# Output weights split in place ahead of the key/value tiles, up's product 5 in front, down's pieces one tile later: a hybrid decoder layer on one core

## The chip, the cores and the metric

The kernel runs on one core of a Trainium2 chip. A core has five engines that each follow their own fixed list of instructions: TensorE (PE; its weight loads are shown apart as PEld), VectorE (DVE), ScalarE (ACT), GpSimd (POOL) and SyncE (SP), which here only issues transfers. ACT and POOL issue transfers too; the three queues are shown as SPq, ACTq and POOLq. An engine stops at an instruction whose inputs or whose buffer aren't ready, and all that stands behind it on that engine waits with it.

The metric is the device time of one execution in microseconds, the median of the runs.

## The reference

One layer of a decoder with two mixers side by side, for 1,024 prompt tokens and 8 samples of 8 new tokens (1,088 tokens in all, model width 1,024).

```python
hn = rms_norm(x, norm_mix_gain)
proj = hn @ w_in                    # q_r k_r v_r g_r (512 each), q_s (512), k_s, v_s (128 each)
o_r = rms_norm(retention(q_r, k_r, v_r)) * silu(g_r)          # 8 heads, chunks of 128
o_s = sliding_window_attention(rms_norm(q_s), rms_norm(k_s), v_s, sinks)   # 8 query, 2 key/value heads
h = x + concat(o_r, o_s) @ w_out
y = h + square(relu(rms_norm(h, norm_ffn_gain) @ w_up)) @ w_down           # width 4096
```

It returns y, the retention states and the last keys and values of the window. All is float32.

## The kernel before

**Precision.** PE multiplies in a shorter form of float32 (`F32R`). So each operand is split into a high part, rounded by an ACT cast, and a low part, the rest, by a DVE subtraction (for a few weights by POOL), and each product is three matmuls: high by high, high by low, low by high (`mm3`, lines 175 to 178; line 176 to 178 are the three matmuls). All matmuls go through this helper, so they have these lines whatever the stage; the stage is told by the PSUM tile's name: `psq`, `pst`, `psf` in the projections, `rsr`, `pm` in retention, `pso` in the output projection, `psx`, `psy`, `psz` in up, `psd` in down. Splits are done by `wload` (input weights, lines 80 and 82), `halve` (line 792 the cast, 793 the subtraction), `split_space` and others.

**Stages, in order of time.** (1) Load of x, its split `hnh`/`hnl`, and the attention queries `psq` (until some 52 us). (2) The keys and values of attention in nine tiles of up to 128 tokens: `pst` is a tile's 24 matmuls of 128x256; ACT squares it (`hsq`), DVE sums per head (`hr`, 315, 316), POOL raises to the power −1/2 (136), DVE scales (318), forms `kn` (320) and copies the values (`q2v`, 335); PE transposes `kn` (`ptk`, 325); ACT and DVE then form the high and low keys `kk`, `kl` (331, 332), two of each for each tile and batch of heads. The last tile gives `v8` and `k8`. (3) Retention's projections (`psf`, from 82 us), attention, retention. (4) The output projection `pso` for two halves of the tokens (s = 0, 1), interleaved with the last tiles of retention, from some 370 us. (5) The MLP: up in 16 column tiles (fp = 0 to 15) by a Strassen-like scheme with seven products, whose left sides are sums of weight blocks (formed by POOL, split by ACT and DVE) and whose right sides are sums of blocks of the normalised h (`f`, `op`); then down by the same kind of scheme (from 870 us).

**The output weights.** `wo_pair` loads two of the eight row blocks of `w_out` at a time for one half of the columns, 512 KB, into a slot of the ring "raw", and splits each half block into a slot of the ring "wa". Each block is needed in both halves of the tokens, so the whole of `w_out` is loaded and split twice: 16 loads, 32 casts and 32 subtractions.

**Up's first tile.** Four of the seven left sides are split while the output projection still runs (`ready`). `PROD = (1, 2, 6, 5, 7, 4, 3)` is the order of the splits and, with an exception for fp = 0, of the products.

**Down's pieces.** Four of down's weight blocks are split ahead, during up: for fp = 3 to 10, `split_down` loads half a block (tile `pw`, 128 KB) behind the last store of up's result, casts and subtracts it in place, and stores it to scratch.

**What sets the order.** The code says what is computed; a scheduler with a timeline model of its own then places the instructions on each engine's list. `tc.issue_after(x)` tells it to place an instruction behind x. PE, DVE, ACT, POOL and SP run the lists as they stand. A tile pool hands out its slots in a ring, and a new tile's first writer waits for the last reader of the slot.

## Time and profile before

| | |
|---|---|
| runs | 1186.14 us median of 3 (1183.59 to 1189.11) |
| profiled execution | 1186.29 us, of which the span of the instructions is 1184.4 us |
| granted TensorE clock | 1.00 |
| busy | PE 1168.4 us (99%), DVE 832.2 (70%), ACT 512.0 (43%), POOL 489.6 (41%) |
| transfers | 174.69 MB, mean 147 GB/s |

The page of the profile first gives each engine's busy time; with PE at 99% the rest of the span is a handful of waits. The view of waits gives, for an engine and a line, what it waited for: in total, how many times, the longest. A row of the timeline is start, duration, engine, line, operation, out<-in, shape and count; in brackets stand the idle time before it and what ended that. A row of windows gives each engine's busy time in a stretch, then the granted clock, the share of the 16 DMA engines in use and GB/s. A row of groups has the line, engine, operation, names, shapes and count, then busy us and mean ns of one, then the idle time before them and what ended it. Matmuls overlap: one of 128x272 is shown with 0.29 us, but the next starts 0.12 us later.

### The profile page before, as it was taken

To read this page: it belongs to the slowest core of one execution; us is meant where nothing else is said; L and a number is where in the kernel's file an instruction comes from. 1 tells how busy PE (TensorE), PEld (TensorE's weight loads), DVE (VectorE), ACT (ScalarE), POOL (GpSimd) and SP (SyncE) were. 2 spreads that over 40 slices of the span, in tenths; PEclk is the share of its full clock that TensorE was granted. 3 is DMA by queue.
4 is the path that set the end of the run, shared out by engine and by line. 5 is a ranking of instruction groups with operands and counts; after the bars stand their busy time and mean duration, and the time that the engine had idled before them with its cause. 6 is when DMAs were issued, how large, how long until landed. Compare 5 with 4: busy or idle time off the path is not lost.

```text
span 1184.4 us, 23548 instructions
## 1 busy us (share of the span) xinstructions
PE 1168.4 (99%) x9405; PEld 1123.3 (95%) x9405; DVE 832.2 (70%) x1551; ACT 512.0 (43%) x1060; POOL 489.6 (41%) x393
## 2 busy tenths in 40 slices
PE   8999999999999999999999999999999999999998
PEld 7999988989879899999999999999999999999998
DVE  7556868732258779887757666667688787888676
ACT  8343544553234347644434444444642333333231
POOL 0135334332255542466655656667373142053000
PEclk9999999999999999999999999999999999999999
DMA  6221334333625555343454444434795456442215
GB/s 247 73 62 62 97 105 162 103 118 94 188 72 170 185 180 156 113 156 121 148 176 149 156 162 165 170 123 152 240 381 170 148 165 204 150 159 94 76 59 188
DMA packets 106181, 174.69 MB, mean 147 GB/s; under 512 B 12319, under 2 KB 71647, under 8 KB 105815
## 3 DMA queue, kind: packets, MB, share of 16 engines
q1 hardware_dynamic: 92711, 129.04, 32.6%
q10 hardware_dynamic: 10800, 35.23, 9.0%
q0 software_dynamic: 2560, 8.91, 2.4%
q8 instruction: 74, 1.21, 0.4%
q14 instruction: 36, 0.29, 0.1%
HBM read 117.45 MB, written 55.71 MB: 146 GB/s over the span
## 4 chain that ended last, share of the span: by engine, by line
PE 78%; DVE 6%; DMA 6%; POOL 4%; issue 3%; ACT 2%; SPq 0%; POOLq 0%; DVEq 0%; ACTq 0%
PE psd L177 9%; PE psd L176 9%; PE psd L178 9%; PE psx L176 4%; PE psx L178 4%; PE psx L177 4%; PE pst L176 2%; PE pst L177 2%; PE pst L178 2%; PE psz L176 2%; PE psz L178 2%; PE psz L177 2%; PE psf L176 2%; PE psf L178 2%; PE psf L177 2%
## 5 line engine op out<-in xcount | busy, mean ns | idle before, releaser
L176 PE MATMUL psd<-uh,wd_w 128*128 128x272 f32 x896 | 258.1, 288 | 1.1 <-ACT a L1287 0.8
L177 PE MATMUL psd<-uh,wd_w 128*128 128x272 f32 x896 | 259.2, 289 | 0.0
L178 PE MATMUL psd<-ul,wd_w 128*128 128x272 f32 x896 | 257.7, 288 | 0.0
L176 PEld LDWEIGHTS psd<-uh,wd_w 128*128 128x128 f32 x896 | 169.1, 189 | 1.6 <-ACT a L1287 1.0
L178 PEld LDWEIGHTS psd<-ul,wd_w 128*128 128x128 f32 x896 | 168.6, 188 | 0.0
L177 PEld LDWEIGHTS psd<-uh,wd_w 128*128 128x128 f32 x896 | 168.4, 188 | 0.0
L1290 DVE TENSOR_TENSOR a<-a,psd 128x272 f32<-128x272 f32 x248 | 100.9, 429 | 48.8 <-PE psd L178 48.7
L793 DVE TENSOR_TENSOR wu_w<-wu_s,wu_w 128x512 fp32r<-128x512 f32 x64 | 55.3, 868 | 51.0 <-ACT wu_w L792 50.7
L793 DVE TENSOR_TENSOR ul<-ur,uh 128x1088 fp32r<-128x1088 f32 (+1 forms) x57 | 83.7, 1496 | 6.3 <-ACT uh L792 6.3
L792 ACT CAST wd_w<-wd_s 128x512 fp32r<-128x512 f32 x64 | 37.0, 617 | 116.0 <-PE psd L178 98.4
L176 PE MATMUL psx<-op_0h,wu_w 128*128 128x272 f32 x256 | 74.3, 291 | 1.8 <-ACT m L1142 1.8
L176 PE MATMUL psx<-op_1h,wu_w 128*128 128x272 f32 x256 | 74.3, 290 | 0.5 <-ACT m L1142 0.5
L178 PE MATMUL psx<-op_1l,wu_w 128*128 128x272 f32 x256 | 74.1, 289 | 0.0
L178 PE MATMUL psx<-op_0l,wu_w 128*128 128x272 f32 x256 | 74.1, 289 | 0.0
L177 PE MATMUL psx<-op_1h,wu_w 128*128 128x272 f32 x256 | 73.7, 288 | 0.0
L177 PE MATMUL psx<-op_0h,wu_w 128*128 128x272 f32 x256 | 73.7, 288 | 0.0
L1126 DVE SCALAR_TENSOR_TENSOR m<-m,rsf 128x272 f32<-128x272 f32 x96 | 68.8, 717 | 3.2 <-ACT rsf L915 0.5
L792 ACT CAST uh<-ur 128x1088 fp32r<-128x1088 f32 (+1 forms) x57 | 59.7, 1085 | 15.0 <-PE psd L177 10.1
L366 POOL TENSOR_TENSOR sp<-sp,ssp 128x1024 f32<-128x1024 f32 (+1 forms) x16 | 28.6, 1788 | 88.4 <-DVE ssp L365 60.0
L176 PE MATMUL psf<-hnh,wqk_hi 128*128 128x384 f32 (+1 forms) x192 | 63.5, 331 | 0.2 <-DVE qkst L518 0.2
L178 PE MATMUL psf<-hnl,wqk_hi 128*128 128x384 f32 (+1 forms) x192 | 63.1, 329 | 0.0
L177 PE MATMUL psf<-hnh,wqk_lo 128*128 128x384 f32 (+1 forms) x192 | 62.8, 327 | 0.0
(345 smaller groups left out, 3618.0 us busy)
## 6 DMA issues: line engine op xcount, KB each, us to landing
ur<-u_d SPq DMA_DIRECT2D x53, 544.0 KB, 5.0
u_d<-r4t SPq DMA_DIRECT2D x32, 544.0 KB, 4.1
wu_r<-in_w_up ACTq DMA_DIRECT2D x32, 512.0 KB, 4.4
wd_r<-in_w_down ACTq DMA_DIRECT2D x30, 512.0 KB, 6.4
u_d<-r3t SPq DMA_DIRECT2D x32, 408.0 KB, 3.0
y<-in_xY POOLq DMA_DIRECT2D x16, 272.0 KB, 3.3
y_d<-y POOLq DMA_DIRECT2D x16, 272.0 KB, 3.4
yt<-y_d SPq DMA_DIRECT2D x16, 272.0 KB, 3.0
```

Source lines behind the costliest of these rows:

```text
L176: nc.tensor.matmul(ps, lh, rh, start=first, stop=False, skip_group_check=more)
L177: nc.tensor.matmul(ps, ll, rh, start=False, stop=False, skip_group_check=more)
L178: return nc.tensor.matmul(ps, lh, rl, start=False, stop=last, skip_group_check=more)
L366: nc.gpsimd.tensor_tensor(s, s, ss.unsqueeze(2).broadcast_to([P, 4, n]), ALU.mult)
L792: nc.scalar.copy(hi, src)
L793: lo_eng.tensor_tensor(lo, src, hi.bitcast(F32), ALU.subtract)
L1126: nc.vector.scalar_tensor_tensor(t_, src, 0.0, rsf[:, s, h, :], ALU.max, ALU.mult)
L1290: added[i] = nc.vector.tensor_tensor(to, to, ps, ALU.add).ins
```

## The change

Three edits.

**1. The output weights.** Each of the eight row blocks is loaded once (512 KB, `load_out`, issued by SP behind the input weight loads) in the stage of the key/value tiles. It is split there (`split_out`): ACT casts the two halves into a free tile, DVE subtracts in place, so that the loaded tile becomes the low part; POOL issues the stores of both to the scratch tensor `wo_d`. The blocks take three slots in turn (rings "s", "pt", "mh", which attention uses later). Blocks 0 to 2 are loaded and split ahead of the tiles; 3, 4, 5, 6 and 7 behind tiles 2, 3, 4, 7 and 8, their casts placed behind that tile's square and their subtractions behind its `kn`. `wq1`'s weights are loaded ahead of the tiles now. In the output projection `wo_pair` loads the split halves, 512 KB for each half block (32 loads instead of 16), into seven slots (four of the ring "wa", three of "raw") and splits nothing.

**2. Up's first tile.** The splits are made in the order 1, 2, 5, 6, 7, 4, 3, and the products in the order (1, 0), (1, 1), (2, 0), (5, 0), (5, 1), (6, 0), (2, 1), (6, 1), where the first number is the product and the second the half of the tokens. The norm of the second half goes behind (6, 0).

**3. Down's pieces.** `split_down` is now a generator: a piece is loaded in one tile of up and cast, subtracted and stored in the next, the cast placed behind the last square of the tile.

```diff
+    def load_out(m):
+        wo_t[m] = sp.tile([P, 4, 256], F32R, tag="s", name=f"wo_raw{m}", bufs=3).rearrange("p k n -> p (k n)")
+        with tc.issue_after(raw_loads[-1].ins):
+            nc.sync.dma_start(wo_t[m].bitcast(F32), a["w_out"][m])
+    def split_out(m, act, dve):
+        lo = wo_t[m]
...
+        for i in range(2):
+            l_ = lo[:, i * 512 : i * 512 + 512]
+            with tc.issue_after(act) if act else ExitStack():
+                nc.scalar.copy(his[i], l_.bitcast(F32))
+            with tc.issue_after(dve) if dve else ExitStack():
+                nc.vector.tensor_tensor(l_, l_.bitcast(F32), his[i].bitcast(F32), ALU.subtract)
+        if m % 3 < 2:
+            nc.gpsimd.dma_start(wo_d[m][:, 0, :], hi.rearrange("p k n -> p (k n)").bitcast(F32))
+        else:
+            for i in range(2):
+                nc.gpsimd.dma_start(wo_d[m][:, 0, i * 512 : i * 512 + 512], his[i].bitcast(F32))
+        nc.gpsimd.dma_start(wo_d[m][:, 1, :], lo.bitcast(F32))
-    w = wload(a["w_in"][2], 8, "wkv", "v")
+    w, w_q1 = (wload(a["w_in"][i], 8, n, "v") for i, n in ((2, "wkv"), (1, "wq1")))
+    for m in range(3):
+        load_out(m)
+    for m in range(3):
+        split_out(m, None, None)
+    for m in range(3, 6):
+        load_out(m)
     for t in range(9):
...
+        m = {2: 3, 3: 4, 4: 5, 7: 6, 8: 7}.get(t)
+        if m:
+            split_out(m, act, dve)
+        if m in (4, 5):
+            load_out(m + 2)
...
     def wo_pair(s, m, half):
-        raw = mw.tile([P, 1024], F32, tag="raw", name=f"wo{half}{s}_{m}_raw", bufs=3)
         c0 = 512 * (half == "a")
-        nc.sync.dma_start(
-            raw.rearrange("p (m n) -> p m n", m=2), a["w_out"][m : m + 2, :, c0 : c0 + 512].rearrange("m p n -> p m n")
-        )
         for i in range(2):
-            yield wsplit(raw[:, i * 512 : i * 512 + 512], "wa", f"wo{half}{s}_{m + i}", nc.vector)
+            tag, bufs = ("raw", 3) if len(w_loads) % 7 > 3 else ("wa", 4)
+            w = mw.tile([P, 2, 512], F32R, tag=tag, name=f"wo{half}{s}_{m + i}", bufs=bufs)
+            w_loads.append(nc.sync.dma_start(w.bitcast(F32), wo_d[m + i][:, :, c0 : c0 + 512]))
+            yield w
...
-                PROD, None, "wu0", nc.vector, tags=("wa", "wa", "wa", "wa", "wb", "wb", "wb"), raws=r0,
+                (1, 2, 5, 6, 7, 4, 3), None, "wu0", nc.vector, tags=("wa", "wa", "wa", "wa", "wb", "wb", "wb"), raws=r0,
...
-            order = [(1, 0), (1, 1), (2, 0), (6, 0), (5, 0)] + [(i, 1) for i in (2, 6, 5)] + order[8:]
+            order = [(1, 0), (1, 1), (2, 0), (5, 0), (5, 1), (6, 0), (2, 1), (6, 1)] + order[8:]
...
-        nc.scalar.copy(w[:, 0, :], w[:, 1, :].bitcast(F32))
+        yield
+        with tc.issue_after(last_sq[0]):
+            nc.scalar.copy(w[:, 0, :], w[:, 1, :].bitcast(F32))
...
+    pieces = chain(*(split_down(f, c) for f in range(2, 6) for c in (0, 256)))
     for fp in range(16):
         up(fp)
-        if 2 < fp < 11:
-            split_down(2 + (fp - 3) // 2, 256 * ((fp - 3) % 2))
+        for _ in range((fp > 2) + (fp > 3)):
+            next(pieces, None)
```

The lines of the changed kernel lie further down: `halve` is at 833 and 834, `split_out` at 327 and 329 with its stores at 331, 334 and 335, the keys at 367 and 368, `kn` at 356, `q2v` at 371, down's cast at 1254.

How the rows move on the engines' lists, at three places. The first is DVE at the end of retention. In the order before, the split of the output weights (`woa`, `wor`) stands ahead of the reduce of a tile's output norm (`orrr`):

```order
L718 TENSOR_TENSOR rptr_4162<-rsr_4155,intra 128x512
L793 TENSOR_TENSOR woa_0_4239<-woa_0_raw,woa_0_4239 128x512
L793 TENSOR_TENSOR wor_0_4244<-wor_0_raw,wor_0_4244 128x512
L754 SCALAR_TENSOR_TENSOR state_3397<-state_3396,decs,pur_4074 64x64 x8
L793 TENSOR_TENSOR woa_1_4342<-woa_0_raw,woa_1_4342 128x512
L793 TENSOR_TENSOR wor_1_4345<-wor_0_raw,wor_1_4345 128x512
L718 TENSOR_TENSOR rptr_4276<-rsr_4269,intra 128x512
L617 TENSOR_REDUCE orrr_4094<-osqr_4092 128x8
```

In the order of the change, at the same place:

```order
L759 TENSOR_TENSOR rptr_4237<-rsr_4230,intra 128x512
L818 TENSOR_TENSOR gt_3979<-pm,gt_3979 128x512
L752 TENSOR_TENSOR qkb<-qt_4335,qkb 64x4x128
L647 TENSOR_TENSOR kdr_4133<-pkr_4128,decs 128x512
L752 TENSOR_TENSOR qkb<-qt_4335,qkb 64x4x128
L759 TENSOR_TENSOR rptr_4246<-rsr_4239,intra 128x512
L658 TENSOR_REDUCE orrr_4178<-osqr_4176 128x8
```

The four splits are gone from between the retention rows.

The second place is DVE in the key/value tiles, around the values of the fifth tile (`pst_810` before). Before:

```order
L315 TENSOR_REDUCE hr_837<-hsq_835 128x2
L316 TENSOR_SCALAR hr_837<-hr_837 128x2
L332 SCALAR_TENSOR_TENSOR kk_570<-ptk_754,c_qkg_111,kk_570 64x128 x2
L318 TENSOR_SCALAR hr_837<-hr_837,rst_180 128x2
L320 TENSOR_TENSOR kn_842<-pst_810,hr_837 128x128
L335 TENSOR_SCALAR q2v_278<-pst_810,rst_180 128x128
L332 SCALAR_TENSOR_TENSOR kl_571<-ptk_754,c_qkg_111,kk_570 64x128
```

Of the change, where the tile is `pst_879` and `wo_raw4` and `wo_raw5` are the fifth and the sixth block of output weights:

```order
L329 TENSOR_TENSOR wo_raw4_679<-wo_raw4_679,wo_hi4_870 128x512 x2
L368 SCALAR_TENSOR_TENSOR kl_579<-ptk_717,c_qkg_111,kk_578 64x128
L351 TENSOR_REDUCE hr_906<-hsq_904 128x2
L368 SCALAR_TENSOR_TENSOR kl_579<-ptk_762,c_qkg_111,kk_578 64x128
L352 TENSOR_SCALAR hr_906<-hr_906 128x2
L351 TENSOR_REDUCE hr_962<-hsq_960 128x2
L352 TENSOR_SCALAR hr_962<-hr_962 128x2
L368 SCALAR_TENSOR_TENSOR kk_578<-ptk_807,c_qkg_111,kk_578 64x128
L354 TENSOR_SCALAR hr_906<-hr_906,rst_188 128x2
L368 SCALAR_TENSOR_TENSOR kk_578<-ptk_859,c_qkg_111,kk_578 64x128
L356 TENSOR_TENSOR kn_911<-pst_879,hr_906 128x128
L371 TENSOR_SCALAR q2v_286<-pst_879,rst_188 128x128
```

Two subtractions stand ahead of the tile's chain, the keys of two tiles are interleaved, and the next two subtractions (block 5) follow this `q2v` directly.

The third place is ACT in up, around the first of down's pieces (`pw2_0`). Before:

```order
L1142 COPY m64_1_7061<-psx1_6951 128x272
L792 CAST wu5_w5_7329<-wu5_s5_7294 128x512
L792 CAST wu5_w3_7432<-wu5_s3_7430 128x512
L1211 CAST pw2_0_6945<-pw2_0_6945 128x256
L1142 COPY m74_0_7107<-psx0_6950 128x272
L1142 COPY m74_1_7124<-psx1_6951 128x272
```

Of the change:

```order
L833 CAST wu5_w4_7412<-wu5_r2_7245 128x512
L1182 COPY m15_0_7262<-psx0_7233 128x272
L1167 ACTIVATE r3t4_1_6974<-v4_1_7177 128x272
L1254 CAST pw2_0_6965<-pw2_0_6965 128x256
L848 DMA wu7_r1_7775<-in_w_up 128x1024
L1167 ACTIVATE r124_0_7199<-m64_0_7064 128x272
```

The cast stood ahead of the copies of product 7 of tile 4; it stands behind that tile's last square now, with a load of up's weights behind it.

More of the change, by code (lines that the diff above doesn't have):

```diff
@@ L64, in cload @@
         return t_
+    raw_loads = []
     def wload(src, kk, name, lo_eng="p", parts=2, after=()):
@@ L73, in wload @@
             for q in range(0, 1024, n):
-                nc.sync.dma_start(raw[:, q : q + n], src[:, h * 1024 + q : h * 1024 + q + n])
+                raw_loads.append(nc.sync.dma_start(raw[:, q : q + n], src[:, h * 1024 + q : h * 1024 + q + n]))
                 if after:
@@ L130, in hymba_layer @@
     ms_lo_d = scratch.tile([P, 4, T], F32, name="ms_lo_d")
+    wo_d = [scratch.tile([P, 2, 1024], F32, name=f"wo_d{m}") for m in range(8)]
     y_d = scratch.tile([P, 4, 4, 2, Q], F32, name="y_d")
@@ L304, in hymba_layer @@
     spread(rst, rsb)
-    w = wload(a["w_in"][2], 8, "wkv", "v")
+    wo_t = {}
+    def load_out(m):
[5 more added lines that the diff above has]
+        if m % 3 < 2:
+            hi = sp.tile([P, 2, 512], F32R, tag="pt", name=f"wo_hi{m}")
+            his = [hi[:, i, :] for i in range(2)]
+        else:
+            his = [sp.tile([P, 512], F32R, tag="mh", name=f"wo_hi{m}_{i}") for i in range(2)]
+        for i in range(2):
[4 more added lines that the diff above has]
+                nc.vector.tensor_tensor(l_, l_.bitcast(F32), his[i].bitcast(F32), ALU.subtract)
+        if m % 3 < 2:
+            nc.gpsimd.dma_start(wo_d[m][:, 0, :], hi.rearrange("p k n -> p (k n)").bitcast(F32))
+        else:
+            for i in range(2):
[8 more added lines that the diff above has]
+        load_out(m)
     for t in range(9):
@@ L312, in hymba_layer @@
         sq = sp.tile([P, 128], F32, tag="hsq", name="hsq")
-        nc.scalar.activation(sq, ps[:, :128], AF.Square, scale=rt)
+        act = nc.scalar.activation(sq, ps[:, :128], AF.Square, scale=rt).ins
         r = sp.tile([P, 2], F32, tag="hr", name="hr")
@@ L319, in hymba_layer @@
         kn = sp.tile([P, 128], F32, tag="kn", name="kn")
-        nc.vector.tensor_tensor(
+        dve = nc.vector.tensor_tensor(
             kn.rearrange("p (h d) -> p h d", h=2), ps[:, :128].rearrange("p (h d) -> p h d", h=2),
             r.unsqueeze(2).broadcast_to([P, 2, 64]), ALU.mult,
-        )
+        ).ins
         pt = psB.tile([P, 512], F32, tag="t2", name="ptk")[:, :128]
@@ L947, in hymba_layer @@
         mix[0, "r" + x] = slot(6 + i, F32R, "mixr" + x)[:, : 8 * Q].rearrange("p (k h n) -> p k h n", k=4, h=2)
-    held, mxr, mxrx = {}, None, ExitStack()
+    held, mxr, mxrx, w_loads = {}, None, ExitStack(), []
     for t in range(5):
@@ L1100, in hymba_layer @@
     um = ux.enter_context(pool("u", side="right"))
-    last_sub, last_store = {}, [None]
+    last_sub, last_store, last_sq = {}, [None], [None]
     def up(fp):
@@ L1147, in up @@
                     act(*wait.pop())
-            if fp == 0 and (i, s) == (5, 0):
+            if fp == 0 and (i, s) == (6, 0):
                 norm(1)
-            if fp == 0 and (i, s) == (5, 1):
+            if fp == 0 and (i, s) == (6, 1):
                 norm_spread(1, mm)
@@ L1158, in up @@
                 squared = act(tq("v", s), bk, s, 0, ra[s][:, B21, :])
+                last_sq[0] = squared.ins
                 nc.sync.dma_start(u_d[fp // 2][:, fp % 2, s, :3, :], ra[s])
```

4 lines of the change are left out of this document (2 added, 2 removed).

## The prediction

> **What bounds the kernel now.** First the page's busy times, then the waits of TensorE (PE), because they say how much there is to win at all.
>
> ```profile
> PE 1168.4 (99%) x9405; PEld 1123.3 (95%) x9405; DVE 832.2 (70%) x1551; ACT 512.0 (43%) x1060; POOL 489.6 (41%) x393
> ...
> PE psx L176 <- ACT m L1142: 2.3, 3, 1.0
> ...
> PE rsr L176 <- ACT qkb L710: 1.2, 1, 1.2
> ...
> PE psz L177 <- DVE wu_w L793: 1.1, 1, 1.1
> ...
> PE pm L772 <- DVE mtr L620: 0.5, 1, 0.5
> ```
>
> PE is busy 1168.4 of 1184.4 us, and the change leaves its matmuls as they are (8,113 PE rows, one fewer). So it can win only waits, and 16 us is all the idle time that there is. Any time it costs has to appear as a new wait of PE. Of the waits listed (us in total, times, longest), the change touches four: L1142, L710, L793 in up, and L620. The others stand in the load phase and in the query projection.
>
> **What it removes.** Three edits, three places.
>
> (1) Down's weight pieces. The two long waits on L1142 have one cause:
>
> ```profile
> 600.62 0.29 PE L178 MATMUL psx<-op_0l,wu_w 128*128 128x272 f32 x1
> ...
> 601.16 0.40 ACT L1211 CAST pw<-pw 128x256 fp32r<-128x256 f32 x1 [4.14 <-DMA pw<-in_w_down]
> 601.47 0.67 ACT L1142 COPY m<-psx 128x272 f32<-128x272 f32 x2
> ...
> 601.91 0.39 PE L176 MATMUL psx<-op_0h,wu_w 128*128 128x272 f32 x1 [1.00 <-ACT m L1142]
> ...
> 665.84 0.40 ACT L1211 CAST pw<-pw 128x256 fp32r<-128x256 f32 x1 [3.98 <-DMA pw<-in_w_down]
> ...
> 666.58 0.39 PE L176 MATMUL psx<-op_0h,wu_w 128*128 128x272 f32 x1 [0.84 <-ACT m L1142]
> ```
>
> ScalarE (ACT) stands 4 us on a load, with the copy that frees PE's bank behind the cast; in the order of before the cast is directly ahead of it. In the change's order the cast stands behind the tile's last square, two products further on (of 24 matmuls, 3 us each). The load takes 2.4 to 7.1 us (view of the tile pw, whose first load is issued at 594.1):
>
> ```profile
> L1210 SPq DMA_DIRECT2D pw<-in_w_down x8: 358/383/383, 594.1 to 745.1; - x8
> ...
> DMA to landing us min/median/max: 2.4/3.8/7.1
> ```
>
> so it has landed, by 601.2 at the latest, when the cast comes at some 606. Removed: 1.00 + 0.84 = 1.8 us of waits. Each wait costs some 0.15 more, because a start after a wait comes late: from 600.62 to 601.91 are 1.29 us where two matmuls of 128x272 otherwise start 0.125 apart (160 in 20 us, window row below), so 1.16 are lost for 1.00 shown. Together 2.1. The third L1142 wait lies at 533, before any piece, and stays.
>
> (2) Up's first tile. PE's fourth group of products waits for a split on VectorE (DVE):
>
> ```profile
> 499.85 0.29 PE L176 MATMUL psz<-op_0h,wu_w 128*128 128x272 f32 x1
> ...
> 500.48 0.68 DVE L793 TENSOR_TENSOR wu_w<-wu_s,wu_w 128x512 fp32r<-128x512 f32 x1
> ...
> 501.21 0.39 PE L177 MATMUL psz<-op_0h,wu_w 128*128 128x272 f32 x1 [1.07 <-DVE wu_w L793]
> ```
>
> That split was the fourth, behind two rounds of out-projection operands. Now product 5 is split third and product 6, split fourth, is read only three groups of twelve matmuls after it (4.5 us). Removed: 1.07 shown, 1.24 by starts (501.21 − 499.85 − 0.12).
>
> (3) The output weights. Today their halves are split beside the retention tail, DVE being nearly full there:
>
> ```profile
> 370.00:390.00 20.00, 19.46 (x213) 18.35 (x213) 18.14 (x32) 9.03 (x16) 10.52 (x7) 1.00 0.57 189
> ...
> 480.00:500.00 20.00, 20.00 (x160) 19.92 (x159) 16.11 (x37) 12.16 (x27) 10.74 (x9) 1.00 0.34 111
> ...
> 375.09 1.78 DVE L793 TENSOR_TENSOR wor<-wor_raw,wor 128x512 fp32r<-128x512 f32 x1
> ...
> 380.67 0.68 DVE L617 TENSOR_REDUCE orrr<-osqr 128x8 f32<-128x512 f32 x1
> ...
> 382.45 2.17 POOL L619 TENSOR_TENSOR orrr<-orrr,mhalf 128x8 f32<-128x8 f32 x1 [3.56 <-DVE orrr L618]
> ...
> 385.40 0.33 PE L772 MATMUL pm<-c_ident,mtr 128*128 128x128 f32 x1 [0.54 <-DVE mtr L620]
> ```
>
> (Columns: PE, PEld, DVE, ACT, POOL busy, granted clock, DMA share, GB/s.) Four of these splits stand ahead of the reduce at 380.67 whose result PE wants at 385.4; without them (one is the row at 375.09; at 0.68, what such a split takes in the row at 500.48, and 1.78 they are 2.7 to 7.1 us of DVE) it comes early enough. The wait at 401.46 follows from the same delay: its load of queries stands on SyncE's queue (SP) behind a load that waits for the previous tile's gate. So 0.54 and 1.17 go, 0.7 and 1.3 by starts.
>
> ```profile
> 400.15 1.26 ACT L710 CAST qkb<-qt 64x512 fp32r<-64x512 f32 x2 [3.00 <-DMA qt<-qr_d]
> 401.46 0.39 PE L176 MATMUL rsr<-qkb 128*128 128x256 f32 x1 [1.17 <-ACT qkb L710]
> ...
> 390.17 0.63 SPq L816 DMA_DIRECT2D mixal<-ms_lo_d  x1
> 390.90 0.57 SPq L547 DMA_DIRECT2D qt<-qr_d  x1
> ```
>
> This query load took 9.2 us from issue (390.90) to the cast (400.15), behind two over four times its size (the second is the row at 390.17); moved some 3 us forward it should land by 397 to 398, when PE still has work. Sum of the gains: 2.1 + 1.24 + 0.7 + 1.3 = **5.4 us**; bounds 3.4 (retention's two stay) and 6.0 (the third L1142 wait, 2.3 − 1.84 = 0.46 and its restart, goes too).
>
> **What it adds.** In the out-projection, 8.4 MB more reading (32 loads of 512 KB for 16) in some 100 us, +84 GB/s:
>
> ```profile
> GB/s 247 73 62 62 97 105 162 103 118 94 188 72 170 185 180 156 113 156 121 148 176 149 156 162 165 170 123 152 240 381 170 148 165 204 150 159 94 76 59 188
> ```
>
> The slices there (29.6 us each, the 14th to the 17th: 185, 180, 156, 113) have room below the 381 of the 30th, and seven slots of 32 are some 20 us of PE's work in hand. Taken as nothing; at worst one load comes as late as the queries' did, 1.3 us.
>
> In the front, 16 casts and 16 subtracts of 128x512, 8 loads and 19 stores. The first three blocks (6 casts, 6 subtracts, 6 x 0.68 = 4.1 us) fall where ACT and DVE stand idle:
>
> ```profile
> 40.64 0.62 DVE L275 TENSOR_SCALAR qs<-psq,qg 128x384 f32<-128x384 f32 x1 [4.74 <-ACT sqq L272]
> 40.12 1.15 ACT L272 ACTIVATE sqq<-psq 128x384 f32<-128x384 f32 x3 [8.49 <-PE psq L178]
> ```
>
> These cost nothing. The other five blocks stand among the key/value tiles, and this is the term that decides. There one tile's product may start only when DVE has drained the product three tiles before (q2v), so I follow DVE from the fourth tile's q2v to the last key (k8), by the order of the change and by the groups of before in 60 to 86 us:
>
> ```profile
> L332 DVE SCALAR_TENSOR_TENSOR kl<-ptk,c_qkg,kk 64x128 fp32r<-64x128 f32 x13 | 4.6, 356 | 2.3 <-ACT kk L331 1.7
> L332 DVE SCALAR_TENSOR_TENSOR kk<-ptk,c_qkg,kk 64x128 fp32r<-64x128 f32 x12 | 4.1, 344 | 1.2 <-issue 0.4 <-ACT kk L331 0.4
> L320 DVE TENSOR_TENSOR kn<-pst,hr 128x128 f32<-128x128 f32 x6 | 1.7, 288 | 0.3
> L315 DVE TENSOR_REDUCE hr<-hsq 128x2 f32<-128x128 f32 x6 | 1.7, 286 | 1.9 <-ACT hsq L313 1.8
> L335 DVE TENSOR_SCALAR q2v<-pst,rst 128x128 f32<-128x128 f32 x5 | 1.7, 342 | 0.0
> L318 DVE TENSOR_SCALAR hr<-hr,rst 128x2 f32<-128x2 f32 x6 | 1.4, 228 | 1.7 <-POOL hr L136 1.6
> L316 DVE TENSOR_SCALAR hr<-hr 128x2 f32<-128x2 f32 x6 | 1.2, 197 | 0.2
> ...
> 60.00:68.00 8.00, 8.00 (x69) 8.00 (x68) 5.51 (x21) 3.53 (x11) 2.09 (x3) 1.00 0.00 0
> ...
> 76.00:84.00 8.00, 8.00 (x52) 7.95 (x51) 5.02 (x16) 3.73 (x11) 4.66 (x3) 1.00 0.43 138
> ```
>
> 14 kl, 12 kk, 5 tiles of reduce, two scalings and kn (0.286 + 0.197 + 0.228 + 0.288 = 1.0 each), 4 q2v, and v and k at 0.35: 5.0 + 4.1 + 5.0 + 1.4 + 0.7 = 16.2 us, and the eight subtracts in between at 0.68 make 21.6. PE's work over the same stretch: three tiles of kv (72 matmuls at 8.00 / 69 = 0.116), two query groups and one key group (72 wider ones at 8.00 / 52 = 0.154), seven transposes at 0.12: 8.4 + 11.1 + 0.8 = 20.3. So the work alone is 1.3 us longer than PE's, where before it was 4.1 shorter. On top come the waits of DVE in this stage, on ACT and GpSimd (POOL), 5.5 us before by the releasers named in these rows (1.7 + 0.4 + 1.8 + 1.6). Bounds: below, the splits fill those waits and DVE enters with a lead, 0; above, all waits remain, 1.3 + 5.5, some 7. I take 4, the middle: half of a fill is what a fixed order with five short chains gives. If one pair took the 1.78 us of the row at 375.09, 2.2 more. The Trainium skill (SBUF — State Buffer, "SBUF: two separate sides") says why some are long: a VectorE operation with two SBUF inputs and a GpSimd operation that reads SBUF exclude each other for a whole instruction. The row at 375.09 agrees; by that rule the subtracts of the last two blocks, beside GpSimd's splits of the key weights, would cost up to 1 us more each.
>
> POOL now issues the stores, nine of them ahead of a tile's reciprocal root (0.70 us). A store of half the size costs its queue 0.74:
>
> ```profile
> L842 POOL DMA_DIRECT2D y_d<-y x16 | 11.8, 736 | 20.3 <-DVE y L840 20.3
> L136 POOL TENSOR_TENSOR hr<-hr,mhalf 128x2 f32<-128x2 f32 x9 | 6.3, 698 | 15.8 <-DVE hr L316 14.1 <-DVE q2v L335 1.7
> ```
>
> At 0.74 nine take 6.7 us of a queue that idles 15.8 before the roots, and they stand in the 4 already. SP's loads of blocks 3 to 7 wait for slots, that is for stores; behind them stand the row scales and a key weight, needed 20 us later.
>
> Sum: 1186.3 (the profiled execution, 0.15 above the median of the three) − 5.4 + 4 = 1184.9, against the median **1184.8 us**, −0.1%.
>
> **Rivals.**
>
> *The front is hidden.* If the eight subtracts fill only DVE's gaps, cost 0 to 1: 1186.2 − 5.4 + 0.5 = 1181.3. For it: DVE is busy only 5.51 and 5.02 of 8 us in the two windows above, so 5.4 us of subtracts find 2.5 to 3 us idle in every 8. Against it: the order puts pairs of subtracts directly ahead of kl and q2v. Chance 0.27.
>
> *Stores block the roots.* If a store of 512 KB holds POOL's queue in proportion to its bytes (0.74 x 512 / 272 = 1.39) or longer, the four that stand in a row ahead of the fifth tile's root cost 2.6 us more and the other five 3.3: 1186.2 − 5.4 + 4 + 5.9 = 1190.7; at three times 0.74 (2.2) the extra is 13 and the time 1198. It decides, against the gains, from about 0.9 us of issue. For it: nothing of this size was stored by POOL before. Against it: on SP's queue a transfer of four times the bytes takes 0.63 where the queries' takes 0.57 (rows at 390). Chance 0.13, at 1192. The Trainium skill (SBUF — State Buffer, the same section) calls it a trap: while VectorE runs in a fast two-port mode, GpSimd can't write its descriptors, and a store of 620 ns takes 3,100. Whether the subtracts (512 elements in 680 ns) are of that kind no run here shows.
>
> *Retention's waits stay*, because the queries' load, still beside the two large ones and now a doubled weight stream, lands as late: 1186.2 − 3.4 + 4 = 1186.8. Chance 0.10.
>
> **How the numbers follow.** Forecast 0.50 (its own range 1182.5 to 1188, from a front of 2 to 7). About 0.5%, 5.9 us, is what a measurement can tell from no change; faster than 1180.2 is then the better half of the hidden front and a little more, 0.18; slower than 1192.1 about 0.10; same 0.72. The range leaves out the far ends of the two outer rivals: 1179.5 to 1191.
>
> **What would show it.** ACT waits nowhere on pw, and no L1142 wait near 600 and 665; no psz wait in up's first tile; none on the mtr or the query cast at 385 and 401; new PE waits between 60 and 92 on q2v, kl, v and k, together near 4 us; POOL's stores near 0.74. PE busy must stay at 1168. Wrong would be a front without waits, stores well above 1 us, or a weight load in the out-projection that PE waits for.

## The result: slower by 1.1%, and the profile after

| | before | change |
|---|---|---|
| median of 6 runs each, on the same chip | 1187.32 us (1183.59 to 1189.11) | 1199.59 us (1197.95 to 1202.1) |
| ratio, with its 95% interval | | 1.011 (1.01 to 1.012) |
| profiled execution, and its span | 1186.29, 1184.4 us | 1202.1, 1200.3 us |
| transfers | 174.69 MB | 195.67 MB |

The change costs 12.3 us where 1.5 us of gain were forecast. Its profiled execution is the slowest of its six; a stretch near 500 us, below, makes most of that difference. One run of e5_only3, below, took 1892 us at a granted clock of 0.56, and the median and the ratio given for it are those of its other ten.

First the busy times and the waits of PE in the profile after (the columns are those of the first fence of the prediction):

```profile
PE 1173.4 (98%) x9405; PEld 1128.3 (94%) x9405; DVE 828.6 (69%) x1535; ACT 505.5 (42%) x1046; POOL 503.6 (42%) x411
...
PE ptk L361 <- DVE kl L368: 6.1, 1, 6.1
PE psr L159 <- DVE acc L897: 4.2, 1, 4.2
PE rsr L181 <- DVE qkb L752: 1.7, 1, 1.7
PE pst L179 <- DVE q2v L371: 1.2, 1, 1.2
...
PE ppp L412 <- DVE ptp L454: 1.2, 1, 1.2
...
PE rsr L179 <- ACT qkb L751: 1.0, 1, 1.0
PE scp L441 <- DVE sp L443: 0.9, 2, 0.7
PE pso L179 <- DVE y L880: 0.8, 1, 0.8
PE psf L179 <- DVE v L376: 0.7, 1, 0.7
...
PE psq L179 <- DVE q2v L371: 0.4, 1, 0.4
```

Three of the four waits that the change was to remove are gone from the list: `psx` on ACT's copies (2.3 us before), `psz` on its split (1.1) and `pm` on `mtr` (0.5). (The third wait on `psx`, near 534, which the prediction let stay, is gone here too; in e1 and e5, below, it stays.) The ten lines shown above make 18.2 us in their place. Those on `q2v` and `v`, 2.3 us together, are the waits that the prediction had named for the key/value tiles. Two single waits are 10.3 us. The one on `kl` stands where the prediction had expected some, but this length was in no term of its sum; the one on `acc` was in no term at all.

To see where the time went, I set PE's matmuls of both profiled executions side by side, row by row, and took the difference of their starts:

| stage | lag of the change, us | grows by |
|---|---|---|
| end of the load phase | −0.7 | |
| after the key/value tiles | 10.2 | 10.9 |
| after attention | 12.9 | 2.7 |
| after retention and output projection | 14.6 | 1.7 |
| after up's first tile | 18.9 | 4.3 |
| after down's pieces | 15.8 | −3.1 |
| end | 15.95 | 0.15 |

The −3.1 are three steps: −0.65 at 534, and −1.26 and −1.11 at 600 and 665 where ACT no longer stands on a piece. The 1.7 of retention and output projection is no more than executions differ by: from the first matmul of retention's values to the last of the output projection before takes 209.3 us (285.9 to 495.2), and e5 and e7, which change nothing there, take 211.4 and 211.9.

### The profile page after: what moved, and what is told of

Read it like the earlier page. It is cut to its first block, busy times and chain, and to the rows that moved or that the text cites. A ratio compares the mean times of both kernels' runs of the same rounds, so it can differ in the third digit from the quotient of the medians.

```text
span 1200.3 us, 23623 instructions
## 1 busy us (share of the span) xinstructions
PE 1173.4 (98%) x9405; PEld 1128.3 (94%) x9405; DVE 828.6 (69%) x1535; ACT 505.5 (42%) x1046; POOL 503.6 (42%) x411
## 2 busy tenths in 40 slices
DMA packets 114021, 195.67 MB, mean 163 GB/s; under 512 B 12991, under 2 KB 72319, under 8 KB 113655
## 4 chain that ended last, share of the span: by engine, by line
PE 78%; DVE 4%; DMA 3%; ACT 1%; issue 1%; POOL 0%; ACTq 0%; DVEq 0%; POOLq 0%; SPq 0%
PE psd L180 9%; PE psd L179 9%; PE psd L181 9%; PE psx L180 5%; PE psx L179 5%; PE psx L181 5%; PE psz L180 3%; PE psz L179 3%; PE psz L181 3%; PE pso L179 2%; PE pso L180 2%; PE pso L181 2%; PE pst L179 1%; PE pst L181 1%; PE pst L180 1%; PE psy L179 1%
## 5 line engine op out<-in xcount | busy, mean ns | idle before, releaser
L834 DVE TENSOR_TENSOR wu_w<-wu_s,wu_w 128x512 fp32r<-128x512 f32 x64 | 59.6, 933 | 50.7 <-ACT wu_w L833 50.0
```

What stands on the lines that cost most here:

```text
L834: lo_eng.tensor_tensor(lo, src, hi.bitcast(F32), ALU.subtract)
```

## The key/value tiles: a load behind a store behind a store

These rows of the timeline of the change show what PE waits for when it stands from 75 to 81 us:

```profile
58.22 0.60 POOL L335 DMA_DIRECT2D wo_d<-wo_raw  x1 [2.67 <-DVE kk L368]
...
66.55 0.34 SPq L174 DMA_DIRECT2D rsb<-r_d  x1
68.25 7.47 SPq L315 DMA_DIRECT2D wo_raw<-in_w_out  x2
...
78.97 1.14 ACT L327 CAST wo_hi<-wo_raw 128x512 fp32r<-128x512 f32 x2 [6.17 <-DMA wo_raw<-in_w_out]
80.13 0.36 ACT L367 ACTIVATE kk<-ptk,c_qkg 64x128 fp32r<-64x128 f32 x1
...
80.53 0.35 DVE L368 SCALAR_TENSOR_TENSOR kl<-ptk,c_qkg,kk 64x128 fp32r<-64x128 f32 x1 [7.08 <-ACT kk L367]
...
74.63 0.27 PE L361 MATMUL ptk<-c_ident,kn 128*128 128x128 f32 x1
81.03 0.45 PE L361 MATMUL ptk<-c_ident,kn 128*128 128x128 f32 x1 [6.13 <-DVE kl L368]
```

Read it from the end. PE's transpose waits for a low key on DVE, which waits for the high key on ACT (80.13). That one stands on ACT's list behind the casts of block 6 of the output weights, and these wait 6.17 us for the block's load. SP issues this load at 68.25, because the block takes the slot of block 3, and the store of block 3's low half, issued by POOL at 58.22, lands only at 68.2. So the store takes 10 us and the load behind it 10.6. The load runs beside the stores that were held up with that one: the core moves 396 GB/s from 72 to 76 us, as the windows below show.

Why does a store of 512 KB take 10 us? The view of transfers, cut to short stretches, shows that the transfer engines move almost nothing then:

```profile
DMA packets 918, 0.00 MB, mean 4 GB/s; under 512 B 918, under 2 KB 918, under 8 KB 918
...
DMA packets 7, 0.03 MB, mean 7 GB/s; under 512 B 0, under 2 KB 0, under 8 KB 7
...
q0 software_dynamic: 7, 0.03, 47.0%
...
wo_d<-wo_hi POOLq DMA_DIRECT2D x1, 512.0 KB, 10.5
```

The first row is 56 to 57 us, the others are 60 to 64 (the third: a queue's packets, MB, and the time that they took as a share of the 16 engines; the last: a store issued there, its size, and its us from issue to landing). The 918 packets are the row scales: 1,088 single words of 4 bytes that SP stores to scratch from 54.92 on (`r_d`, lines 172 and 173 of the change), as the kernel before does. In the kernel before nothing else is issued until they have landed, 12 us later, so that the trace of before shows them as a slow but harmless store. The change issues five stores in these 12 us, and the loads that need what the words or the stores leave come after them.

The standstill costs a second time. From the windows of PE in the change (us, PE busy with its matmuls, granted clock, share of the DMA engines, GB/s):

```profile
72.00:76.00 4.00, 2.90 (x25) 1.00 1.03 396
76.00:80.00 4.00, 0.00 (x0) 0.78 0.60 229
80.00:84.00 4.00, 2.57 (x8) 0.50 0.39 149
84.00:88.00 4.00, 4.00 (x22) 0.87 0.46 140
```

After 6 us without a matmul PE comes back at a granted clock of 0.50 and runs at half rate for some 4 us (until about 85, by the 0.87 of the last row), which loses some 1.6 us more: ten matmuls of 128x384 start 0.32 us apart there, where they start 0.17 apart afterwards. The Trainium skill ("TensorE: Matmul & The Clock Gate", "What's actually happening") says that the array's clock falls to half after an idle window of some 3.4 us, and that a busy window of the same length brings it back; the rows agree. The wait of 4.2 us near 520 does the same (granted clock 0.74 and 0.83 in the two stretches of 4 us from 520 on); no shorter one does in this execution.

## The experiments

Each run is compared with the median of before in its own batch (1186.1, 1186.69 or 1186.79 us for the experiments, 1187.32 for the change). Since these medians differ by 1.2 us, differences between batches below 1 us mean nothing.

| run | what | us (runs) | against before | ratio, 95% |
|---|---|---|---|---|
| the change | all three edits | 1199.59 (6) | +12.3 | 1.011, 1.01 to 1.012 |
| e2_front_only | loads and splits of the output weights as before, on top of the new front | 1199.37 (4) | +13.3 | 1.0105, 1.0085 to 1.0124 |
| e3_ring4 | the change, four slots for seven | 1196.84 (4) | +10.7 | 1.008, 1.0058 to 1.0102 |
| e4_rd_rows | the change, row scales stored as rows | 1192.93 (6) | +6.8 | 1.0053, 1.0037 to 1.007 |
| e8_nosub | e4 without ten subtractions (it leaves out forming five blocks' low parts) | 1193.35 (1) | +6.7 | |
| e9_mended | change with rows, four slots, up's first tile as before | 1188.35 (10) | +1.6 | 1.0012, 1.0002 to 1.0021 |
| e1_only23 | edits 2 and 3 alone | 1185.4 (10) | −0.7 | 0.9989, 0.9978 to 1.0 |
| e5_only3 | edit 3 alone | 1184.95 (10) | −1.7 | 0.9985, 0.9974 to 0.9996 |
| e7_wq1 | before, `wq1` loaded ahead | 1187.94 (1) | +1.3 | |
| e6_probe, e10_probe_load | before, with transfers behind the single words | 1188.61, 1185.21 (1 each) | +1.9, −1.6 | |
| r1_again | the change once more | 1199.09 (1) | +12.3 | |

### The edits taken apart: e1_only23, e2_front_only, e3_ring4

e1 has edits 2 and 3 on the kernel before, without the output weights. e2 is the change with its output projection put back:

```diff
+        raw = mw.tile([P, 1024], F32, tag="raw", name=f"wo{half}{s}_{m}_raw", bufs=3)
...
-            tag, bufs = ("raw", 3) if len(w_loads) % 7 > 3 else ("wa", 4)
-            w = mw.tile([P, 2, 512], F32R, tag=tag, name=f"wo{half}{s}_{m + i}", bufs=bufs)
-            w_loads.append(nc.sync.dma_start(w.bitcast(F32), wo_d[m + i][:, :, c0 : c0 + 512]))
-            yield w
+            yield wsplit(raw[:, i * 512 : i * 512 + 512], "wa", f"wo{half}{s}_{m + i}", nc.vector)
```

e3 is the change with `tag, bufs = "wa", 4` for all loads.

> The second and third edits alone (up's first tile and down's pieces), the output weights as before. The forecast's terms say 2.1 us for the pieces and 1.24 for product 5, so 3.3 us faster than before: the waits on the copy near 600 and 665 and the one on the split near 500 are gone, nothing else moves. The rival, that these waits only move to another place of up, gives 0 to 1 us. If the gain is 3 or more, all that the change loses (12 us, or 15 with this gain) comes from the output weights.

> The change, but the output projection loads and splits its weights as before; the splits and stores in front stay, and nothing reads what they store. It parts the loss of the first edit into the front and the later stages. By the two traces the front (52 to 100 us) loses some 10 to 11 us, retention some 2 and the start of up 4. Theory: this kernel keeps the front's loss and drops the other two, so it is about 6 us faster than the change and about 6 slower than before. Rival: the late losses follow from the front (other order on the engines) and not from the doubled loads and the slots; then it is as slow as the change.

> The change with four slots for the split output weights instead of seven; the three slots of the ring raw are left to up's first weight loads, as before. Theory on the wait of 4.2 us of TensorE on the sum of squares near 517 us: up's raw loads came at 491.9 and 494.9 us instead of 471 and 479, because their slots held output weights until TensorE had used them, so GpSimd's sum of weight blocks came at 500 instead of 488 and the residual loads behind it on GpSimd's queue with it. Then this kernel has no such wait and is 4 us faster than the change. Second effect: six loads of 512 KB instead of seven or more stand ahead of the key and query loads of retention, so the waits near 400 us (3 us) get shorter. Rival: the residual loads are late because the doubled stream slows every load; then the wait near 517 stays, and four slots make new waits for weights in the output projection, 2 us or more.

e1 settles that the whole loss comes with edit 1: without it the kernel is level with before. (Edit 1 alone was not run.) It gained less than the 3.3 us that the prediction's terms had promised. The pieces' two waits are gone, and so is the 1.24 us wait in up's first tile. But in the same tile two new ones stand, 1.07 us (`psr` on `acc`, the norm of the second half) and 0.72 us (`psx` on a copy of ACT): edit 2 moved the wait instead of removing it. On e2 I was wrong by 6 us: with the loads and splits of before the kernel is no faster than the change. Its profile has the same 5.4 us wait on `kl` at 74 us and the same growth in attention, and the wait for the query cast is 2.0 us. So the output projection's new loads don't make the loss. e3 gave 1.6 to 2.8 us where 4 were expected; its profile lacks the long wait on `acc` (0.37 us are left of it), which is taken up again below.

### The row scales: e4_rd_rows

PE transposes the scales first, and they go out as nine rows, eight of 512 bytes and one of 256, instead of 1,088 words:

```diff
-        nc.sync.dma_start(r_d[0:1024].rearrange("(t p) -> p t", p=128), rst[:, :8])
-        nc.sync.dma_start(r_d[1024:1088].rearrange("(p t) -> p t", t=1), rst[64:128, 8:9])
+        ps = psB.tile([P, 512], F32, tag="t2", name="psrow")[:9, :128]
+        nc.tensor.transpose(ps, rst[:, :9], ident)
+        rows = nt.tile([P, 512], F32, tag="ntmp", name="rstrow")[:9, :128]
+        nc.vector.tensor_copy(rows, ps)
+        nc.sync.dma_start(r_d[0:1024].rearrange("(t p) -> t p", p=128), rows[:8, :])
+        nc.sync.dma_start(r_d[1024:1088].unsqueeze(0), rows[8:9, 64:128])
```

> The change with one other thing: the row scales are transposed on TensorE and stored as nine rows of 512 bytes instead of 1,088 single words of 4 bytes. In the change's trace five stores of output weights issued from 58.2 to 64.4 us land only at 68 to 75, and the memory is all but idle from 57 to 66 (7 GB/s in 60 to 64); before them the store of single words was issued at 54.9. Before, that store takes 12.3 us from issue to landing. Theory: single words hold up the writes behind them for some 10 us; block 6's load waits for a slot, that is for such a store, and lands at 78.9, where ScalarE's cast of it stands ahead of the keys of the tiles. Then the stores here land within 6 us, ScalarE doesn't wait 6 us for block 6, TensorE's wait of 6.1 us near 75 and the half clock behind it are gone: 8 to 10 us faster than the change. Rival one: GpSimd's own queue is slow to give out its stores; then they land as late as now, and the time stays. Rival two: the memory is full there; the same.

The change's excess fell from 12.3 to 6.8 us, and in the two profiles the lag at the end of the key/value tiles from 10.2 to 3.6. That is less than the 8 to 10 expected: I had counted the front's whole lag. (e4's load phase ends 0.9 us ahead of before's, so its tiles still cost 4.5.) The timeline of SP in this run:

```profile
57.73 0.35 SPq L176 DMA_DIRECT2D r_d<-rstrow  x1
58.14 0.22 SPq L177 DMA_DIRECT2D r_d<-rstrow  x1
59.32 0.35 SPq L178 DMA_DIRECT2D rsb<-r_d  x1
65.07 6.99 SPq L319 DMA_DIRECT2D wo_raw<-in_w_out  x2
```

The load at line 178 reads what the two rows above it store, so they have landed 1.6 us after the first was issued; as words they took 12 us (before) and 11 (the change: 55.4 to 66.55). The store of block 3 now lands in 5.4 us, block 6's load is issued at 65.07 instead of 68.25 and has landed at 71.8 instead of 78.9. ACT's cast stands as before behind a tile's square and ahead of a key, and waits 0.28 us instead of 6.17; first its row, then two of PE's windows of this run:

```profile
71.91 1.14 ACT L331 CAST wo_hi<-wo_raw 128x512 fp32r<-128x512 f32 x2 [0.28 <-DMA wo_raw<-in_w_out]
...
76.00:80.00 4.00, 4.00 (x25) 1.00 0.38 125
80.00:84.00 4.00, 3.56 (x25) 1.00 0.65 201
```

The two windows in which PE stood or ran at half rate have 4.00 and 3.56 us of matmuls now, at the full clock. So the late transfer and its half clock cost 5.5 us by the medians and 6.6 by the profiles. The other way out, to keep the words and cast block 6 behind the keys, was not tried.

### Is it the words? e6_probe and e10_probe_load

On the kernel before, which has nothing behind the words, three transfers of 512 KB were put behind them, a store and a load on POOL's queue and a store on SP's:

```diff
...
+        if t == 2:
+            for v in (pa, pb, pc):
+                nc.gpsimd.tensor_tensor(v[:, 0:2], r, r, ALU.add)
+            nc.gpsimd.dma_start(pb, a["w_out"][1])
+            nc.gpsimd.dma_start(probe_d[0], pa)
+            nc.sync.dma_start(probe_d[1], pc)
```

and in e10 the load `pb` alone.

> The kernel before with three probes right behind the store of the 1,088 single words (issued at 55): a store of 512 KB on GpSimd's queue, a store of 512 KB on SyncE's queue, and a load of 512 KB on GpSimd's queue. What they move is used nowhere. Theory (single words hold up the writes to memory behind them, whatever queue these come from): both stores land only when the words have, 66 to 70 us, some 10 us after their issue, and the load, which only reads memory, lands within 4 us. Rival one, GpSimd's queue is slow: its store and its load are late, SyncE's store isn't. Rival two, all transfers wait: the load is late too. Rival three, GpSimd's stores were late in the change because of the amount stored: all three land within 6 us here.

> The kernel before with one probe behind the store of the 1,088 single words: a load of 512 KB on GpSimd's queue, alone. In the run with three probes the load landed as late as the two stores (71 us, 13 us after its issue), but it stood behind GpSimd's own store. Theory: single words hold up only the writes to memory; alone, the load lands in 3 to 5 us, as such loads do elsewhere. Rival: they hold up reads as well; then it lands at 68 or later, 10 us or more after its issue.

The last row of each view of a tile gives the time from issue to landing, shortest, median, longest. In e6 the tile `probea` (a load at the kernel's start, then the store on POOL's queue), `probec` (the same, with the store on SP's) and `probeb` (the load):

```profile
DMA to landing us min/median/max: 5.9/9.2/12.5
...
DMA to landing us min/median/max: 7.2/9.2/11.2
...
DMA to landing us min/median/max: 13.1/13.1/13.1
```

and the load alone, in e10:

```profile
L321 POOL DMA_DIRECT2D probeb<-in_w_out x1: 734/734/734, 55.7 to 55.7; - x1
...
DMA to landing us min/median/max: 11.7/11.7/11.7
```

All four come 11 to 13 us after their issue, at 67 to 71 us, and the store on SP's queue is as late as the one on POOL's. My theory before e10 was that only writes queue behind the words; it fell, a load by itself is as late. So the words hold up what is issued behind them, loads and stores on POOL's queue and stores on SP's, and it isn't one queue that is slow. (ACT's queue was not tried, nor whether it is the words' size or their number.) What it is that they hold is open: by the trace of the change their packets are over by 57 us, and of the transfers behind them only 7 packets of 4 KB start between 60 and 64. These take 47% of the 4 us of 16 engines, which is 4.3 us each; in e4 the 375 packets from 61 to 65 take 0.17 us each. The Trainium skill ("DMA: Bandwidth & Descriptors", "Specifications") names 512 bytes as the smallest transfer that reaches the full rate, and a read-modify-write below it; eight of e4's nine rows have that size, and the run agrees in direction.

### What is left of the front: e8_nosub and e7_wq1

```diff
                 nc.scalar.copy(his[i], l_.bitcast(F32))
+            if m > 2:
+                continue
             with tc.issue_after(dve) if dve else ExitStack():
```

(on e4), and on the kernel before `wq1`'s weights loaded together with the key/value weights, as the change does.

> The change with the row scales stored as rows, as in the run that was 6.7 us faster than the change, and without the ten subtractions of the output weights' blocks 3 to 7 (so these blocks' low parts are the whole weights: the output projection computes something else, at the same cost). The forecast gave the subtractions among the tiles 4 us; with the rows six waits of 0.3 to 1.0 us are left there, 4.4 in all. If the subtractions on VectorE make them, they go to 1 us or less and the front is as in before. If they come from the order of TensorE (transposes of two tiles together) or from ScalarE's casts, at least 3 us of them stay.

> The kernel before, with one of the change's small moves: the second query weights are loaded and split ahead of the key/value tiles in the code. In the change's trace the stage of the attention (100 to 300 us) loses 2 to 2.5 us in three waits that before has not: 0.9 near 129 on DVE's sp, 1.3 near 249 on ptp, 0.5 near 258 on sp. If this move makes them (another order in attention), they are here at the same places and this is 2 us slower than before; if they follow from the splits and stores among the tiles, the profile is that of before.

Without the ten subtractions the front's lag is 2.0 us smaller than e4's, and three waits of 0.39, 0.62 and 0.73 us stay, where e4 has five of 0.46 to 0.73. So neither expectation held: of the 4.5 us which e4 left in the tiles the subtractions are some 2, and the rest stays. That the rest comes from the casts, the stores and the order that they bring is not shown. It is one execution each, so give or take some tenths. The total did not fall (1193.35), because this run had the long wait on `acc` that e4 nearly lacked: 5.25 against 1.28 us.

A part of the subtractions' price is the neighbour. In the profile of the change:

```profile
81.65 5.17 POOL L84 TENSOR_TENSOR wqk_lo<-wqk_raw,wqk_hi 128x1024 fp32r<-128x1024 f32 x2 [0.68 <-ACT wqk_hi L82]
...
82.10 5.27 DVE L329 TENSOR_TENSOR wo_raw<-wo_raw,wo_hi 128x512 fp32r<-128x512 f32 x2
...
L329 DVE TENSOR_TENSOR wo_raw<-wo_raw,wo_hi x16: 673/684/2872, 34.9 to 92.7; 128x512 fp32r<-128x512 f32 x16
```

Two subtractions take 2.6 us each beside POOL's splits of key weights, where the median of the sixteen is 0.684. This fits the rule that the prediction cited from the Trainium skill (SBUF — State Buffer, "SBUF: two separate sides"), and here they take 2 us more each, where I had allowed 1.

e7's profile has none of attention's new waits. So the 2.7 us there don't come from `wq1`'s earlier load; all runs with the new front have them (0.9 us at `scp`, 1.2 at `ppp`), down to e9. They don't come from the ten subtractions either, since e8 has them in full, nor from the words (e4) or the output projection (e2). What is left is the casts, the loads and the stores, and the order that the scheduler gave; these were not parted.

### Up's first tile: r1_again beside the change

> The change unchanged, for a second profile. Its first profile was of the slowest of its six runs (1202.1 against a median of 1199.6). Theory: the waits that hang on the order of the engines and on block 6's load come again to within 0.5 us (6 us near 75, 1.3 near 249, 3 near 402); the wait near 517, at the end of a chain of loads on GpSimd's queue, varies, and is 1 to 3 us instead of 4.4. Rival: it is as long as before, and the run to run difference lies elsewhere.

The same kernel again, and the long wait on `acc` is not there. Up's first tile then loses nothing against before, where the profiled execution of the change lost 4.3; the span is 3.0 us shorter, 1197.3. The other waits came again, 5.5 us on `kl`, 1.2 on `ptp` and 2.8 on the query cast and its subtraction. Another 1.6 us were lost among the matmuls of retention's values, where the granted clock of this execution is 0.50 from 322 to 324. Timelines of POOL and PE, of the change first:

```profile
500.25 5.41 POOL L1121 TENSOR_TENSOR wu_s<-wu_r 128x512 f32<-128x512 f32 x1 [3.83 <-DMA wu_r<-in_w_up]
505.61 0.56 POOL L878 DMA_DIRECT2D y<-in_xY  x1
...
521.70 0.69 PE L159 MATMUL psr<-ones,acc 128*32 128x1 f32 x48 [4.20 <-DVE acc L897]
```

and of the repeat:

```profile
500.13 1.28 POOL L1121 TENSOR_TENSOR wu_s<-wu_r 128x512 f32<-128x512 f32 x1 [1.70 <-DMA wu_r<-in_w_up]
502.01 0.55 POOL L878 DMA_DIRECT2D y<-in_xY  x1 [0.60 <-DMA y_d<-y]
...
518.46 0.58 PE L159 MATMUL psr<-ones,acc 128*32 128x1 f32 x48
```

The first of POOL's sums of up's weights takes 5.41 us in one execution and 1.28 in the other. It runs beside DVE's subtractions, and behind it on POOL's list stands the load of a residual (`y<-in_xY`), which goes out 3.6 us later. DVE waits for that residual before it can finish the norm, and PE's `psr` comes 3.2 us later. e8 and e4 make two more points:

```profile
490.37 6.15 POOL L1127 TENSOR_TENSOR wu_s<-wu_r 128x512 f32<-128x512 f32 x1 [4.09 <-DMA wu_r<-in_w_up]
...
512.61 0.82 PE L159 MATMUL psr<-ones,acc 128*32 128x1 f32 x48 [5.25 <-DVE acc L903]
```

```profile
493.72 1.72 POOL L1125 TENSOR_TENSOR wu_s<-wu_r 128x512 f32<-128x512 f32 x1 [4.13 <-DMA wu_r<-in_w_up]
...
511.43 0.58 PE L159 MATMUL psr<-ones,acc 128*32 128x1 f32 x48 [1.28 <-DVE acc L901]
```

Sums of 1.28, 1.72, 5.41 and 6.15 us go with waits of 0, 1.28, 4.20 and 5.25. The sum takes over 5 us in the kernel before and in e1 too (5.72 and 5.71), with one residual's load behind it; there PE waits 0 and 0.91 us. In the change two residuals come behind it. Three of edit 1's seven slots are those of up's first raw weights, whose loads are issued at 492 and 495 instead of 471 and 479; 14.5 us of that is the lag of the whole kernel at this point, so the first is some 6 us late against PE and the second 1. With four slots (e3, e9) no sum stands between these residuals, and 0.37 us and nothing are left of the wait. So slots and sum are shown to belong to it; that the sum's length alone decides between the executions is read from four of them.

### The change mended: e9_mended

e4's rows, e3's four slots, and edit 2 taken back.

> The change with the three things mended that the runs so far found: the row scales stored as rows, four slots for the output weights, and up's first tile in the order of before; down's pieces stay as in the change. Theory, by the terms measured so far against before: key/value tiles +3.4 (subtractions among the tiles and the order of the transposes), attention +2.8, retention +0.5 to +1, up's start 0, pieces -2.4, so 4 to 5 us slower than before, 1190 to 1191.5. If so, the moved splits cost more than they free even without the late block. Rival: the terms hang together (a mended front also mends attention's order), and the gains show: at or below before.

1188.35 us, 2 to 3 us better than expected, and still 1.6 slower than before (by an interval that just excludes no change). The profile adds up: key/value tiles +4.7 us, attention +2.7, retention 0, up's first tile −1.2, down's pieces −2.4. (Its profiled execution is the slowest of the ten.) Take away edit 3, which is worth 1.7 by e5, and edit 1 costs some 3 us even where its accidents are mended. What it was to bring does not come: the waits in retention and the output projection are 0.34, 1.08 and 1.02 us by starts, 2.4 together, where before has 0.70 and 1.33.

### The best version: e5_only3

> The third edit alone, on the kernel before: down's pieces are cast one tile later. The second and third together measured 1.3 us faster than before, not 3.3; in their profile the pieces give 2.4 us, while up's first tile has two new waits (1.07 on the sum of squares, 0.72 on a copy) for the one removed (1.24). Theory: the third edit is worth 2.1 to 2.4 us alone and the second nothing or a loss, so this is 1184, 2.1 to 2.4 us faster than before and 0.5 to 1 us faster than both together. Rival: the second edit is worth its 1.2 us and the third less; then this is no faster than both together.

Down's pieces alone: 1184.95 us, 0.15% faster than before, with an interval that just excludes no change (0.04% to 0.26%), and 14 us faster than the change. That is 1.7 us, less than the 2.1 to 2.4 expected, and the traces tell why. The waits that the edit removes differ from execution to execution. Three more executions have the pieces in the order of before, and PE waits there 0.46 (e6), 0.80 (e7) and not at all (e10) near 600, and 0.55, not at all and 0.87 near 665. With the 1.00 and 0.84 of before the four make 1.1 us on average; the prediction had read the one with the most. The cast comes where the prediction had put it, and a load is waited for by nobody:

```profile
606.02 0.38 ACT L1142 COPY m<-psx 128x272 f32<-128x272 f32 x1
...
606.62 0.40 ACT L1214 CAST pw<-pw 128x256 fp32r<-128x256 f32 x1
```

## Why the prediction was wrong, step by step

**What held.** The pieces, by their mechanism: the cast at "some 606" stands at 606.62, and both waits are gone. The size, 2.1 us forecast, is −1.26 and −1.11 in the profile, 2.4 together, but the medians of e5 give 1.7, with 0.5 to 3.1 as the interval: the term was read from one execution in which the waits were long. The rival of the stores that block the roots was rightly set aside: the stores on POOL were issued in 0.53 to 0.72 us each (they are 18 and not 19, and both profiles have 9,405 rows of PE where the prediction counted 8,113 and one fewer). The front's term for the key/value tiles, 4 within 0 to 7, was right in size: 4.5 us in e4, where the transfers are in time. That is luck in part, because the prediction laid it to DVE, and e8 gives DVE's subtractions some 2 of it.

**The step that failed** is the sentence "SP's loads of blocks 3 to 7 wait for slots, that is for stores; behind them stand the row scales and a key weight, needed 20 us later". It asked what stands behind these loads on SP's queue and priced the answer at nothing. It did not ask who waits for the loads themselves. Block 6's cast stands ahead of a key on ACT's list. The chain is store, slot, load, cast, key, transpose, and its first link, the store, was never given a duration. Measured: a 6.13 us wait and some 1.6 us lost at half clock. e4 took 5.5 to 6.6 us of the loss away.

The words themselves could have been seen. The trace of before shows `r_d` issued at 55.0 and the load that reads it at 67.5; a store of 4 KB that takes 12 us, in the stretch into which the change puts stores, is the row to stop at. What it does to others no row of before could show, since nothing else moves there; bounded from that row, between nothing and those 12 us, it would have taken the range to 1197 (an estimate, 1184.9 + 12).

**Up's first tile, 1.24.** The wait went and came back as 1.07 and 0.72 (e1, by starts). Its size varies too: with the order of before it is 0.57 to 1.07 us as shown in five executions (before, e5, e6, e7, e10), and in e9 it isn't there. I had followed the split that was late, and not the norm and the copy that were next.

**"Seven slots of 32 are some 20 us of PE's work in hand"** looked at the slots only as room for the output weights. Three of them belong to up, and by them POOL's sum came ahead of the last residuals: 0 to 5 us, by how long that sum takes in an execution.

**Retention, 0.7 and 1.3.** Both waits named went. For another tile's queries others came:

```profile
400.35 1.26 ACT L751 CAST qkb<-qt 64x512 fp32r<-64x512 f32 x2 [2.68 <-DMA qt<-qr_d]
401.65 0.19 PEld L179 LDWEIGHTS rsr<-qkb 128*128 128x128 f32 x1 [1.20 <-ACT qkb L751]
401.65 0.39 PE L179 MATMUL rsr<-qkb 128*128 128x256 f32 x1 [0.98 <-ACT qkb L751]
...
404.09 0.39 PE L181 MATMUL rsr<-qkb 128*128 128x256 f32 x1 [1.70 <-DVE qkb L752]
```

The queries of this tile are issued at 390.57, behind the keys (383.41) and seven loads of output weights of 512 KB each (379.3 to 385.7), and land 9.7 us later. The doubled reading, "taken as nothing; at worst one load comes as late as the queries' did, 1.3 us", cost 3.0 by starts here (1.14 and 1.86). It isn't the amount read: with four slots (e3, e9) as much is read, but four loads stand ahead of the keys and none between them and the queries, and neither wait is in the list. So what costs is the loads that three more slots let go ahead. With the old loads (e2) the wait of before is back at its old place, behind `mixah` and `mixal`, with 2.0 us. The rival that retention's waits stay came near this mechanism, and had 2.0 us for its price.

**Attention** was in no step. Its 2.7 us come with edit 1's front, and how they arise stays open.

## What to carry to other kernels

When a load is moved behind a store, follow the slot: who frees it, when that store really lands in this stretch of the program, and what stands behind the consumer of the load on the consumer's engine. A store of many single words was slow here, and so was what was issued behind it; make rows of it before putting transfers there. A wait read from one execution can be the longest of several: where the unchanged code can be run again, look at it in more than one trace before pricing its removal. And removing 5 us of small waits on an engine that is 99% busy is worth little when the edit puts a chain of six links, each with its own delay, among tiles in which DVE had 4 us to spare.

## What the runs showed of the hardware

- Single words hold up other transfers. 1,088 stores of 4 bytes, whose packets end within some 2 us, delay stores of 512 KB on POOL's and SP's queues and loads on POOL's to 11 to 13 us (e6, e10; stores in the change 10). The same bytes as nine rows land within 1.6 us (e4), and a store behind them in 5.4.
- A 128x512 sum on POOL takes 1.28 us or over 5, in the same place of the same kernel, and with it a wait of PE is 4.2 us or none (the change and its repeat, whose spans differ by 3.0). The long ones run beside DVE's subtractions. That the two exclude each other for a whole instruction, as the Trainium skill says (SBUF — State Buffer, "SBUF: two separate sides"), fits both these rows and the 2.6 us subtractions; which of the two holds the other up, no run tells.
- Six us without a matmul leave PE at half clock for its next 4 us, which adds about a quarter to the wait; 4.2 us without one cost some 1.5 us more in the same way. The half clock also came with no wait of PE ahead of it, for some 3.4 us among retention's values: granted clock 0.50 in 322 to 324 in r1_again and in 310 to 312 in e5 and e7, at 1.6 us each. No run shows why.
